# Even mixer reordered, output-norm sums moved to GpSimd, and a chunk-by-chunk first tile, in an eight-core decoder step

## The chip, the cores and the metric

The kernel runs as one program on all 8 NeuronCores of one Trainium2 chip (two dies, cores 0 to 3 and 4 to 7). Each core handles one prompt sequence of 2048 tokens and 16 sampled sequences of 8 tokens; nothing is exchanged between cores. The metric is the device time of the slowest core in microseconds (us), lower is better. Every execution also lists each core's span (first to last instruction) and the mean clock that the throttle granted to its TensorE.

Executions are labelled fast or slow. Slow means that one die was over 1% longer than the other at a lower clock, or that the run was over 1.5% above the fastest of the same kernel.

## The reference, cut to what matters

A trunk of two layers. Both have two SwiGLU half-steps and a gated per-layer embedding; layer 0 has the "even" mixer, layer 1 the "odd" one (a short gated convolution).

```python
def even_mixer(h, ...):
    proj = h @ w_in                     # xa (512) | va (512) | ga (512)
    pooled = causal_multiscale_pool(xa) # trailing means of 2, 4, 8, 16 rows, minus the row
    pa = einsum(pooled, pool_proj) * pool_scale
    u = va * sigmoid(ga)
    yb = silu(layernorm(causal_depthwise_conv(u, 31 taps) + dw_bias))
    return concat([pa, yb]) @ w_out
# for each layer
x = x + 0.5 * swiglu(rmsnorm(x), ...)
x = x + mixer(rmsnorm(x))
x = x + 0.5 * swiglu(rmsnorm(x), ...)
x = x + sigmoid(rmsnorm(x) @ w_ple_gate) * rmsnorm(p @ w_ple_proj)
```

## The kernel before

The tokens of a core are five blocks: 0 to 3 of 512 prompt tokens, and the "sample" block SB of 128. X (fp32), H (normed input, bf16) and the weights' ring stay in SBUF. The program is written in one stream: `defer(t, f)` puts work off until an estimated TensorE time, `ensure(tag)` runs what is pending now, and a scheduler derives the semaphores. `bank` hands out PSUM banks, `scr` and `SQ` hand out scratch. Cuts are marked with `# ...`.

```python
class Norm:                                # sums of squares of X for the next RMSNorm
    def chunk(self, mo, lag=0.8):          # called once for each of the 8 chunks of a block
        def square():
            if self.mode == "dve" and mo == 0:
                self.acc = scr(); act(self.acc, xs, AF.Square); return
            sq = SQ.get()
            act(sq, xs, AF.Square)
            defer((2.0 if self.mode == "pe" else 1.2) * k, lambda: add(sq), self.tag)
        def add(sq):                       # "pe": a matmul with ones; "dve": an add on VectorE
            # ...
            elif mo < 7:
                dve_tt(self.acc, self.acc, sq, ALU.add); SQ.put(sq)
            else:
                dve_tt(sq, self.acc, sq, ALU.add); sfree(self.acc)
                defer(2.5 if n == 512 else 9.0, lambda: stats(sq), self.tag)   # one matmul

def out_proj(b, src, wo, gnext):           # of both mixers
    nm = Norm(b, gnext)                    # mode "dve"
    for mo in range(8):
        pb = bank()
        mm(pb, [(wo[mo][:, k, :], src[b][:, k, :]) for k in range(8)])
        dve_tt(X[b][:, mo, :], pb, X[b][:, mo, :], ALU.add)
        nm.chunk(mo)

# inside even_mixer
def load_r(b):      # 16 DMAs: copies of u, shifted by 0 to 3 rows, for the convolution ("rr")
    # ... queue "act" if b > 1 and q % 2 else "sp"
def pp(b):          # pool_proj: one matmul a channel group, then a copy on ScalarE into H
    for c in range(4):
        mm(pb, [(wpp[:, c, :], H[b][:, c, :])])
        act(H[b][:, c, :], pb, AF.Copy, scale=pcol("pool_scale", c))

for b in (0, 1, 2, SB, 3):
    for j in range(4):
        vg(j, b)                           # value and gate, u
    xa(b)                                  # pool input; windowed sums on VectorE, 9 us a block
    # b == 0: load_r(0), states
    if b == SB:
        conv(0)
        load_r(1)
for b in range(NB):
    if b + 1 < NB:
        conv(b + 1)                        # conv + casts + LayerNorm statistics
    pp(b)
    if b + 2 < NB:
        load_r(b + 2)
    out_proj(b, H, wo, gnext)

# the start of the program
# X[0] on two queues; weight tile 0 waits for X chunk 2; X[1] waits for weight tile 2
for c in range(8):
    raw[0].chunk(c, "dve")                 # H = X * gain (unscaled), squares, statistics by matmul
def chunk1(c):
    raw[1].chunk(c, "pool")                # H of block 1 on GpSimd
for c in range(8):
    defer(9.5 + 0.75 * c, lambda c=c: chunk1(c), ("raw", 1))
# ffn then runs tiles 0..3 of block 0, tiles 0..3 of block 1, and so on
```

## Time and profile before

| | before |
|---|---|
| median of 4 runs | 2684.82 us (2683.16 to 2687.39) |
| profiled execution | 2663.17 us, slowest core 2661.4 |
| TensorE busy | 97% of the span |
| spans of the eight cores in the profiled execution | 2651.0 to 2661.4 us |

The page of the profile gives each engine's busy time (us, share of the span, instructions) and the chain of waits that ended last, as shares of the span by engine.

```profile
PE 2586.6 (97%) x14375; PEld 1249.3 (47%) x14375; DVE 1187.5 (45%) x2144; ACT 704.6 (26%) x1250; POOL 99.6 (4%) x174
...
PE 85%; DVE 8%; ACT 3%; issue 1%; DMA 1%; ACTq 0%; POOL 0%; SPq 0%; DVEq 0%; POOLq 0%
```

TensorE is busy for 97% of the span and is 85% of the chain, so it is the bottleneck: only its idle time and its time at a lower clock can be won back. Its timeline for the start of the slowest core (core 6) shows start, duration, operation, and in brackets the idle time before it with what ended it:

```profile
6.21 0.59 PE L547 MATMUL ps<-sq_88,ones 128*128 128x512 bf16 x1 [6.21 <-DVE h_48 L714]
...
15.94 14.53 PE L547 MATMUL ps<-h_48,ring 128*128 128x512 bf16 x56 [2.17 <-DMA ring<-wts]
...
34.25 0.39 PE L547 MATMUL ps<-sq_88,ones 128*128 128x512 bf16 x1 [0.48 <-ACT sq_88 L510]
38.81 3.59 PE L547 MATMUL ps<-h_49,ring 128*128 128x512 bf16 x8 [4.18 <-POOL h_49 L714]
...
60.20 1.90 PE L547 MATMUL ps<-h_50,ring 128*128 128x512 bf16 x8 [1.81 <-DVE h_50 L520]
```

Block 0's first tile begins at 15.94 us, when its weights have landed. Block 1 (h_49) waits 4.18 us for GpSimd's last chunk. Block 2 (h_50) is reached at 60.20 us.

The same view for the even mixer:

```profile
590.26 2.48 PE L547 MATMUL ps<-h_52,ring 128*128 128x128 bf16 x24 [3.39 <-DVE scr_95 L520]
...
632.52 1.04 PE L547 MATMUL ps<-pt_75,onesl 128*128 128x512 bf16 x2 [3.14 <-DVE pt_75 L534]
...
641.22 3.63 PE L547 MATMUL ps<-h_48,ring 128*128 128x512 bf16 x16 [1.64 <-ACT h_48 L510]
...
667.83 5.31 PE L547 MATMUL ps<-h_49,ring 128*128 128x512 bf16 x16 [1.98 <-ACT h_49 L510]
...
696.04 5.31 PE L547 MATMUL ps<-h_50,ring 128*128 128x512 bf16 x16 [2.08 <-ACT h_50 L510]
...
715.84 0.28 PE L547 MATMUL ps<-pt_75,onesl 128*128 128x128 bf16 x2 [2.24 <-DVE pt_75 L534]
...
721.60 3.60 PE L547 MATMUL ps<-h_51,ring 128*128 128x512 bf16 x8 [1.89 <-ACT h_51 L510]
...
741.93 6.44 PE L547 MATMUL ps<-h_52,ring 128*128 128x128 bf16 x64 [3.19 <-ACT h_52 L510]
```

Here TensorE waits for the sample block's gating on VectorE (scr_95), three times for casts of the convolution's output (pt_75; one of them, 0.84 us, is not shown), and before each output projection for ScalarE's pool copies (h_48 to h_52).

### The profile page before, as it was taken

To read this page: it belongs to the slowest core of one execution; us is meant where nothing else is said; L and a number is where in the kernel's file an instruction comes from. 1 tells how busy PE (TensorE), PEld (TensorE's weight loads), DVE (VectorE), ACT (ScalarE), POOL (GpSimd) and SP (SyncE) were. 2 spreads that over 40 slices of the span, in tenths; PEclk is the share of its full clock that TensorE was granted. 3 is DMA by queue.
4 is the path that set the end of the run, shared out by engine and by line. 5 is a ranking of instruction groups with operands and counts; after the bars stand their busy time and mean duration, and the time that the engine had idled before them with its cause. 6 is when DMAs were issued, how large, how long until landed. Compare 5 with 4: busy or idle time off the path is not lost.

```text
span 2661.4 us, 34887 instructions; the slowest of 8 cores (2651.0 to 2661.4 us)
## 1 busy us (share of the span) xinstructions
PE 2586.6 (97%) x14375; PEld 1249.3 (47%) x14375; DVE 1187.5 (45%) x2144; ACT 704.6 (26%) x1250; POOL 99.6 (4%) x174
## 2 busy tenths in 40 slices
PE   7999999999899999999999999999999999999997
PEld 2444544443354444444444454445444444544443
DVE  3432434765742222248832222257568322222587
ACT  5210112325531101124521001123333210011254
POOL 2000000000000000000000000000000000000000
PEclk9999999999899999999999999999999999999999
DMA  9220421145322204213032121202320221322113
GB/s 205 42 41 4 64 44 25 33 88 116 85 44 37 44 9 71 44 25 49 8 56 44 25 45 32 44 13 37 50 46 16 49 44 25 46 46 40 21 22 135
DMA packets 53312, 127.19 MB, mean 48 GB/s; under 512 B 9504, under 2 KB 24608, under 8 KB 53024
## 3 DMA queue, kind: packets, MB, share of 16 engines
q0 software_dynamic: 23584, 92.55, 21.4%
q1 hardware_dynamic: 25392, 27.90, 3.7%
q10 hardware_dynamic: 4176, 4.50, 0.7%
q8 instruction: 113, 1.85, 0.3%
q14 instruction: 47, 0.39, 0.0%
HBM read 196.61 MB, written 10.62 MB: 78 GB/s over the span
## 4 chain that ended last, share of the span: by engine, by line
PE 85%; DVE 8%; ACT 3%; issue 1%; DMA 1%; ACTq 0%; POOL 0%; SPq 0%; DVEq 0%; POOLq 0%
PE ps L547 85%; DVE h_50 L520 1%; ACT L508 1%; DVE h_51 L520 1%; DMA ring<-wts 1%; DMA xscr_69<-st_sc 0%; DVE x_46 L520 0%; DVE h_49 L520 0%; DVE v L516 0%; DVE h_48 L520 0%; DVE x_45 L520 0%; DVE x_43 L520 0%; DVE scr_97 L516 0%; DVE scr_96 L516 0%; DVE scr_96 L520 0%
## 5 line engine op out<-in xcount | busy, mean ns | idle before, releaser
L547 PE MATMUL ps<-h_49,ring 128*128 128x512 bf16 x1892 | 430.9, 382 | 6.2 <-POOL h_49 L714 4.2
L547 PE MATMUL ps<-h_48,ring 128*128 128x512 bf16 x1892 | 430.9, 382 | 6.1 <-DVE x_47 L516 2.3
L547 PE MATMUL ps<-h_50,ring 128*128 128x512 bf16 x1892 | 427.9, 380 | 5.3 <-ACT h_50 L510 2.1
L547 PE MATMUL ps<-h_51,ring 128*128 128x512 bf16 x1892 | 429.7, 381 | 2.0 <-ACT h_51 L510 1.9
L547 PEld LDWEIGHTS ps<-h_49,ring 128*128 128x128 bf16 x1892 | 185.8, 98 | 231.9 <-issue 5.2
L547 PEld LDWEIGHTS ps<-h_50,ring 128*128 128x128 bf16 x1892 | 185.3, 98 | 230.6 <-ACT h_50 L510 2.6
L547 PEld LDWEIGHTS ps<-h_51,ring 128*128 128x128 bf16 x1892 | 185.6, 98 | 227.4 <-issue 3.5
L547 PEld LDWEIGHTS ps<-h_48,ring 128*128 128x128 bf16 x1892 | 182.2, 98 | 211.9 <-issue 8.1
L571 POOL DMA_DIRECT2D ring<-wts x152 | 81.0, 540 | 2297.0 <-PE ps L547 2248.5
L547 PE MATMUL ps<-hid_54,ring 128*128 128x512 bf16 x736 | 163.7, 379 | 0.0
L547 PE MATMUL ps<-hid_55,ring 128*128 128x512 bf16 x736 | 163.7, 379 | 0.0
L547 PE MATMUL ps<-hid_56,ring 128*128 128x512 bf16 x736 | 163.7, 379 | 0.0
L547 PE MATMUL ps<-hid_53,ring 128*128 128x512 bf16 x736 | 162.8, 379 | 0.0
L510 ACT ACTIVATE scr_97<-ps 128x512 f32<-128x512 f32 (+1 forms) x128 | 72.7, 568 | 265.4 <-PE ps L547 263.4
L510 ACT ACTIVATE scr_95<-ps 128x512 f32<-128x512 f32 (+1 forms) x116 | 59.8, 515 | 311.1 <-PE ps L547 307.2
L510 ACT ACTIVATE scr_93<-ps 128x512 f32<-128x512 f32 (+1 forms) x128 | 73.6, 575 | 250.7 <-PE ps L547 240.3
L547 PE MATMUL ps<-h_52,ring 128*128 128x128 bf16 x1892 | 126.7, 223 | 9.7 <-DVE scr_95 L520 3.4
L547 PEld LDWEIGHTS ps<-h_52,ring 128*128 128x128 bf16 x1892 | 117.1, 100 | 32.5 <-DVE scr_95 L520 3.6
L510 ACT ACTIVATE scr_94<-ps 128x512 f32<-128x512 f32 (+1 forms) x108 | 54.3, 503 | 234.8 <-PE ps L547 229.7
L510 ACT ACTIVATE scr_96<-ps 128x512 f32<-128x512 f32 (+1 forms) x125 | 59.0, 472 | 207.6 <-PE ps L547 200.5
L547 PEld LDWEIGHTS ps<-hid_54,ring 128*128 128x128 bf16 x736 | 72.0, 98 | 86.9
L547 PEld LDWEIGHTS ps<-hid_56,ring 128*128 128x128 bf16 x736 | 72.1, 98 | 86.6
(474 smaller groups left out, 2161.5 us busy)
## 6 DMA issues: line engine op xcount, KB each, us to landing
ring<-wts POOLq DMA_DIRECT2D x110, 512.0 KB, 9.0
ring<-wts POOLq DMA_DIRECT2D x40, 768.0 KB, 7.9
rr<-u SPq DMA_DIRECT2D x36, 135.0 KB, 3.1
x_44<-xT SPq DMA_DIRECT2D x8, 256.0 KB, 5.8
x_45<-xT SPq DMA_DIRECT2D x8, 256.0 KB, 7.9
x_46<-xT SPq DMA_DIRECT2D x8, 256.0 KB, 9.5
yT<-x_43 SPq DMA_DIRECT2D x8, 256.0 KB, 2.1
yT<-x_44 SPq DMA_DIRECT2D x8, 256.0 KB, 2.1
```

The costliest lines, as they stand in the source:

```text
L508: e.preload_act_table_set(tset)
L510: return e.activation(out=out, in_=in_, func=func, **kw)
L520: S.op("dve", lambda e: e.scalar_tensor_tensor(out=out, in0=in0, scalar=scalar, in1=in1, op0=op0, op1=op1), reads=rd, writes=[out])
L547: ins = e.matmul(o_, l, r, start=st, stop=sp)
L571: S.op(eng, lambda e: e.dma_start(out=out, in_=in_), reads=[in_], writes=[out], dma_sem=sem, dma_total=total, extra_deps=extra)
```

## The change

Its intent: put VectorE's backlogs under projections that don't need them, take the norm sums of the output projections off VectorE, and start the first tile as X arrives.

```diff
@@ Norm: a third mode, sums on GpSimd; statistics in "pe" mode put off longer
+            self.wait = {"pe": 4.0, "dve": 1.2, "pool": 1.0}[mode]
+            add_tt = pool_tt if self.mode == "pool" else dve_tt
-                defer((2.0 if self.mode == "pe" else 1.2) * k, lambda: add(sq), self.tag)
+                defer(self.wait * k, lambda: add(sq), self.tag)
-                    dve_tt(self.acc[:, 0:n], self.acc[:, 0:n], sq[:, 0:n], ALU.add)
+                    add_tt(self.acc[:, 0:n], self.acc[:, 0:n], sq[:, 0:n], ALU.add)
@@ out_proj
-        nm = Norm(b, gnext)
+        nm = Norm(b, gnext, "dve" if b == SB else "pool")
@@ RawNorm.chunk: H of blocks 0 and 1 both on VectorE; squares kept in HID, statistics after the tile
-            S.op(eng, lambda e: e.tensor_scalar(out=H[b][:, c, :], ...
+            dve_ts(H[b][:, c, :], X[b][:, c, :], pcol(self.gname, c), ALU.mult)
@@ ffn: first tile of blocks 0 and 1 chunk by chunk
+                if rw is not None and pi == 0 and j == 0:
+                    for k in range(8):
+                        mm_ops([(pg[:, 0:n], wt[:, k, 0:128], H[b][:, k, :], k == 0, k == 7),
+                                (pu[:, 0:n], wt[:, k, 128:256], H[b][:, k, :], k == 0, k == 7)])
+                    rw.stats()
@@ even_mixer: load_r all on one queue, weights of pp loaded before diag, and this order
-        for b in (0, 1, 2, SB, 3):   ... vg, xa; conv(0), load_r(1) after SB
-        for b in range(NB):          ... conv(b + 1), pp(b), load_r(b + 2), out_proj(b)
+        vgs(0); xa(0); load_r(0)     # calls set on one line here
+        vgs(1); pp(0); xa(1)
+        vgs(2); pp(1)
+        vgs(SB); xa(2); xa(SB)
+        vgs(3, (0, 1)); conv(0); load_r(1); vgs(3, (2, 3))
+        xa(3); pp(2); pp(SB)
+        for b in range(NB):
+            if b + 1 < NB:
+                conv(b + 1)
+                if b + 2 < NB:
+                    load_r(b + 2)
+            if b == 0:
+                pp(3)
+            ensure(("ln", b))
+            out_proj(b, H, wo, gnext)
@@ start: weight tile 0 first; X[1] behind weight tile 1; tile order
-    W.extra[0] = (("x0_2", 0, 16),)
+    W.extra[1] = (("x0_3", 0, 16),)
+    W.extra[3] = (("x1_2", 0, 16),)
+    first = [(0, 0), (1, 0), (2, 0), (0, 1), (1, 1), (2, 1), (3, 0), (3, 1)]   # (tile, block)
```

More of the change, by code (lines that the diff above doesn't have):

```diff
@@ L77, in weight_tile_list @@
                 tiles.append((("ine_xa", j), 8 * 256))
+            tiles.append((("pp",), 4 * 128))
             tiles.append((("diag",), 16 * 8 * 32))
-            tiles.append((("pp",), 4 * 128))
             for ch in TRI:
@@ L516, in dve_tt, with pool_tt @@
         S.op("dve", lambda e: e.tensor_tensor(out=out, in0=in0, in1=in1, op=op), reads=[in0, in1], writes=[out])
+    def pool_tt(out, in0, in1, op):
+        S.op("pool", lambda e: e.tensor_tensor(out=out, in0=in0, in1=in1, op=op), reads=[in0, in1], writes=[out])
     def dve_stt(out, in0, scalar, in1, op0, op1):
@@ L592, in __init__ @@
             self.extra = {}
-            self.limit = 4
         def _place(self, k):
@@ L613, in _place, with pump @@
             return None if best is None else (best[1], u)
-        def pump(self):
-            while self.pos < self.limit:
+        def pump(self, limit=1 << 20):
+            while self.pos < min(limit, len(self.order)):
                 k = self.order[self.pos]
@@ L645, in __init__ @@
             self.tag = ("n", b)
-            self.pb = None
+            self.nsq = self.nadd = 0
+            self.wait = {"pe": 4.0, "dve": 1.2, "pool": 1.0}[mode]
         def chunk(self, mo, lag=0.8):
@@ L650, in chunk @@
             k = 1.0 if n == 512 else 0.4
+            add_tt = pool_tt if self.mode == "pool" else dve_tt
             def square():
-                if self.mode == "dve" and mo == 0:
+                self.nsq += 1
+                if self.mode != "pe" and self.nsq == 1:
                     self.acc = scr()
@@ L658, in square @@
                 act(sq[:, 0:n], xs, AF.Square)
-                defer((2.0 if self.mode == "pe" else 1.2) * k, lambda: add(sq), self.tag)
+                defer(self.wait * k, lambda: add(sq), self.tag)
             def add(sq):
+                i = self.nadd
+                self.nadd += 1
                 if self.mode == "pe":
-                    if mo == 0:
+                    if i == 0:
                         self.pb = bank()
-                    mm(self.pb[:, 0:n], [(ONES[:, :], sq[:, 0:n])], start=mo == 0, stop=mo == 7)
+                    mm(self.pb[:, 0:n], [(ONES[:, :], sq[:, 0:n])], start=i == 0, stop=i == 7)
                     SQ.put(sq)
-                    if mo == 7:
+                    if i == 7:
                         self.rsqrt()
-                elif mo < 7:
-                    dve_tt(self.acc[:, 0:n], self.acc[:, 0:n], sq[:, 0:n], ALU.add)
+                elif i < 6:
+                    add_tt(self.acc[:, 0:n], self.acc[:, 0:n], sq[:, 0:n], ALU.add)
                     SQ.put(sq)
                 else:
-                    dve_tt(sq[:, 0:n], self.acc[:, 0:n], sq[:, 0:n], ALU.add)
+                    add_tt(sq[:, 0:n], self.acc[:, 0:n], sq[:, 0:n], ALU.add)
                     sfree(self.acc)
-                    defer(2.5 if n == 512 else 9.0, lambda: stats(sq), self.tag)
+                    defer({512: 2.5, NSAMP: 9.0}[n] + (1.5 if self.mode == "pool" else 0.0), lambda: stats(sq), self.tag)
             def stats(sq):
@@ L708, in __init__, with chunk, stats, lead_order @@
             self.rs = RSB[b]
-            self.pb = None
-        def chunk(self, c, eng):
+        def chunk(self, c):
             n, b = self.n, self.b
-            col = pcol(self.gname, c)
-            S.op(eng, lambda e: e.tensor_scalar(out=H[b][:, c, :], in0=X[b][:, c, :], scalar1=col, scalar2=None,
-                                                op0=ALU.mult), reads=[X[b][:, c, :], col], writes=[H[b][:, c, :]])
-            sq = SQ.get()
+            sq = HID[SB - 1 - b][:, c, :]
+            dve_ts(H[b][:, c, :], X[b][:, c, :], pcol(self.gname, c), ALU.mult)
             act(sq[:, 0:n], X[b][:, c, :], AF.Square)
-            def add():
-                if c == 0:
-                    self.pb = bank()
-                mm(self.pb[:, 0:n], [(ONES[:, :], sq[:, 0:n])], start=c == 0, stop=c == 7)
-                SQ.put(sq)
-                if c == 7:
-                    act(self.rs[:, 0:n], self.pb[:, 0:n], AF.Abs_reciprocal_sqrt, bias=NORM_EPS)
-                    bfree(self.pb)
-            defer(1.6, add, ("raw", b))
-    def lead_order(nt, lead):
-        out = []
+        def stats(self):
+            n = self.n
+            pb = bank()
+            mm(pb[:, 0:n], [(ONES[:, :], HID[SB - 1 - self.b][:, c, 0:n]) for c in range(8)])
+            act(self.rs[:, 0:n], pb[:, 0:n], AF.Abs_reciprocal_sqrt, bias=NORM_EPS)
+            bfree(pb)
+    def lead_order(nt, lead, first=None):
+        out = list(first or [])
         for b in range(NB):
-            out += [(t, b) for t in range(min(lead, nt))]
+            out += [(t, b) for t in range(min(lead, nt)) if (t, b) not in out]
         for t in range(lead, nt):
@@ L790, in emb_stats, with ffn @@
         defer(0.6, s0, tag)
-    def ffn(l, f, gnext, lead=3, raw=()):
+    def ffn(l, f, gnext, lead=3, raw=(), first=None, arrive={}):
         for pi, part in enumerate(HPARTS):
@@ L796, in ffn @@
                     load_pt(l, b, b)
-            order, last = lead_order(len(part), lead if pi == 0 else 0)
+            order, last = lead_order(len(part), lead if pi == 0 else 0, first if pi == 0 else None)
             for oi, (j, b) in enumerate(order):
@@ L804, in ffn @@
                 pg, pu = bank(), bank()
-                mm(pg[:, 0:n], [(wt[:, k, 0:128], H[b][:, k, :]) for k in range(8)])
-                mm(pu[:, 0:n], [(wt[:, k, 128:256], H[b][:, k, :]) for k in range(8)])
+                pe_t[0] = max(pe_t[0], arrive.get((pi, j, b), 0.0))
+                if rw is not None and pi == 0 and j == 0:
+                    for k in range(8):
+                        mm_ops([(pg[:, 0:n], wt[:, k, 0:128], H[b][:, k, :], k == 0, k == 7),
+                                (pu[:, 0:n], wt[:, k, 128:256], H[b][:, k, :], k == 0, k == 7)])
+                        pe_t[0] += 2 * (n + 6.5) / 2400.0
+                    rw.stats()
+                else:
+                    mm(pg[:, 0:n], [(wt[:, k, 0:128], H[b][:, k, :]) for k in range(8)])
+                    mm(pu[:, 0:n], [(wt[:, k, 128:256], H[b][:, k, :]) for k in range(8)])
                 sg = scr()
@@ L885, in load_r @@
                         src = US[32 * q:32 * q + 32, :, s * NS:s * NS + L]
-                    items.append(("act" if b > 1 and q % 2 else "sp", RALL[32 * s:32 * s + 32, :, q, 0:L], src))
+                    items.append(("sp", RALL[32 * s:32 * s + 32, :, q, 0:L], src))
             dma_group(items, "rsem")
@@ L1029, in state, with vgs @@
                 dma("sp", V[:, :, 0:15 * NS], d_stp[:, :, :], "stp")
-        for b in (0, 1, 2, SB, 3):
+        def vgs(b, js=range(4)):
             ensure(("n", b))
@@ L1034, in even_mixer @@
                 ensure(("us",))
-            for j in range(4):
+            for j in js:
                 vg(j, b)
-            xa(b)
-            if b == 0:
-                dve_memset(RALL[96:128, :, :, 536:RW], 0.0)
-                load_r(0)
-                for j in range(4):
-                    defer(3.0 * j, lambda j=j: state(j), ("us",))
-                dma("sp", d_o_ps[:, :, 0:7 * NS], d_stp[:, :, 8 * NS:15 * NS], "osem")
-                dma("sp", d_o_ds[:, :, 0:22 * NS], d_stdw[:, :, 8 * NS:30 * NS], "osem")
-            if b == SB:
-                conv(0)
-                load_r(1)
+        vgs(0)
+        xa(0)
+        dve_memset(RALL[96:128, :, :, 536:RW], 0.0)
+        load_r(0)
+        for j in range(4):
+            defer(3.0 * j, lambda j=j: state(j), ("us",))
+        dma("sp", d_o_ps[:, :, 0:7 * NS], d_stp[:, :, 8 * NS:15 * NS], "osem")
+        dma("sp", d_o_ds[:, :, 0:22 * NS], d_stdw[:, :, 8 * NS:30 * NS], "osem")
+        wpp = kview(W.get(("pp",)), 4)
+        vgs(1)
+        pp(0)
+        xa(1)
+        vgs(2)
+        pp(1)
+        vgs(SB)
+        xa(2)
+        xa(SB)
+        vgs(3, (0, 1))
+        conv(0)
+        load_r(1)
+        vgs(3, (2, 3))
+        for j in range(4):
+            W.done(("ine_vg", j))
+        xa(3)
+        W.done(("ine_xa", 0))
+        W.done(("ine_xa", 1))
         dve_ts(O_DP[:, :, :], O_DP[:, :, :], 0.5, ALU.mult)
@@ L1050, in even_mixer @@
         dma("sp", d_o_pp[:, :, :], PTAIL[:, :, 1:16], "osem")
-        for j in range(4):
-            W.done(("ine_vg", j))
-        W.done(("ine_xa", 0))
-        W.done(("ine_xa", 1))
-        wpp = kview(W.get(("pp",)), 4)
+        pp(2)
+        pp(SB)
         wo = out_tiles("oute")
@@ L1059, in even_mixer @@
                 conv(b + 1)
-            else:
+                if b + 2 < NB:
+                    load_r(b + 2)
+            if b == 0:
+                pp(3)
+                W.done(("pp",))
+            if b + 1 == SB:
                 W.done(("diag",))
-            pp(b)
-            if b + 2 < NB:
-                load_r(b + 2)
             ensure(("ln", b))
             out_proj(b, H, wo, gnext)
-        W.done(("pp",))
         for ch in TRI:
@@ L1148, in ple @@
             W.done(("pleg", l, ch))
+    W.pump(1)
     dma("act", PAR[:, :], d_par[:, :], "psem")
@@ L1155, in build_program @@
             dma("act" if b == 0 and c % 2 else "sp", X[b][:, c, :], d_xT[:, o_:o_ + n], f"x{b}_{c}",
-                extra=(("wsem4", 0, 16),) if b == 1 and c == 0 else ())
-    W.extra[0] = (("x0_2", 0, 16),)
+                extra=(("wsem2", 0, 16),) if b == 1 and c == 0 else ())
+    W.extra[1] = (("x0_3", 0, 16),)
+    W.extra[3] = (("x1_2", 0, 16),)
     W.extra[4] = tuple((f"x{SB}_{c}", 0, 16) for c in range(8))
-    dve_memset(ONES[:, :], 1.0 / D)
+    W.pump()
     raw = [RawNorm(b, "norm_ffn00") for b in range(2)]
     for c in range(8):
-        raw[0].chunk(c, "dve")
-        pe_t[0] += 0.8
-        run_due()
-    pe_t[0] = 11.5
+        raw[0].chunk(c)
+        if c == 0:
+            dve_memset(ONES[:, :], 1.0 / D)
     dve_memset(ONESL[:, :], 1.0 / 512)
@@ L1170, in build_program, with at_time @@
         dve_memset(RC[:, t:t + 1], 1.0 / (t + 1))
-    W.pump()
-    def chunk1(c):
-        raw[1].chunk(c, "pool")
-        if c == 7:
-            W.limit = len(wtiles)
-            W.pump()
+    pe_t[0] = 9.4
+    def at_time(t, fn, tag):
+        defer(t - pe_t[0], fn, tag)
     for c in range(8):
-        defer(9.5 + 0.75 * c, lambda c=c: chunk1(c), ("raw", 1))
+        at_time(19.5 + 0.87 * c, lambda c=c: raw[1].chunk(c), ("raw", 1))
     n0 = [Norm(b, "norm_ffn00", "pe" if b < SB else "dve") for b in range(NB)]
     for b in range(2, NB):
+        n0[b].wait = 1.5
         for mo in range(8):
-            defer((16.0, 24.0, 32.0)[b - 2] + (0.7, 0.9, 0.5)[b - 2] * mo, lambda b=b, mo=mo: n0[b].chunk(mo, 0.0), ("n", b))
+            at_time((27.0, 37.0, 47.0)[b - 2] + (0.8, 1.0, 0.5)[b - 2] * mo,
+                    lambda b=b, mo=mo: n0[b].chunk(mo, 0.0), ("n", b))
+    first = [(0, 0), (1, 0), (2, 0), (0, 1), (1, 1), (2, 1), (3, 0), (3, 1)]
+    arrive = {(0, 1, 0): 15.5, (0, 2, 0): 18.5, (0, 3, 0): 28.5}
     for l in range(2):
-        ffn(l, 0, f"norm_mix{l}", lead=4 if l == 0 else 3, raw=raw if l == 0 else ())
+        if l == 0:
+            ffn(l, 0, f"norm_mix{l}", lead=4, raw=raw, first=first, arrive=arrive)
+        else:
+            ffn(l, 0, f"norm_mix{l}")
         if l == 0:
```

## The prediction

The forecast's sum came to 11 + 24 + 3 = 38 us (steps 1 to 3), less some for a wait not foreseen, and gave 2650 us.

> **What bounds it now.** TensorE: busy 97% of 2661.4 us on the slowest core and 85% of the chain that ended last. So the change can win back only TensorE's idle and half-clock time. At the warm start-to-start time of 0.216 us per 512-column matmul (0.056 for 128 columns) all matmuls need about 2560 us; some 89 us on this core is lost, by the matmuls' starts: 26.6 us before 80 us, 40.1 in the even mixer (500 to 770 us; 33 to 45 over the cores), 9.4 around 1300 us (untouched), 8.3 in and after the odd output projection, 12.1 at the end (untouched).
>
> - Start (timeline of TensorE): first matmul at 6.21, statistics matmuls until 13.2, weights at 15.94, a 4.18 us wait for POOL's h_49 at 38.81; block 2 starts at 60.20.
> - Mixer: 0.52 and 3.39 us for the sample's evacuations behind VectorE's work on xa(2); 0.84, 3.14, 2.24 us for the convolution's casts; 1.64, 1.98, 2.08, 1.89, 3.19 us for ScalarE's pool copies h_48..h_52 right before each out_proj. Together 20.9 us.
> - Clock: long gaps are followed by 3.4 to 10 us at 0.5. [...] 34 us of it in the mixer, costing up to half that.
>
> **What the change does.**
> 1. Start: weights first; gate and up matmuls follow each X chunk; statistics after the tile. First tile done near 13.5 instead of 20 us. H of block 1 moves from POOL (1604 ns a chunk) to VectorE (about 0.5 us). Block 2 should start near 48 us. Gain about 11 us.
> 2. Mixer: pp(b) no longer stands directly before its out_proj: its 10.8 us of waits go, with their half clock. The sample's projections precede xa(2): 3.9 us go. But conv(0) now follows xa(2) and xa(sample), about 9 + 6 us of VectorE work over 9 us of TensorE work, and conv(1) still follows xa(3) closely: I expect 2 to 4 us of wait for casts at each. Loss 37 to about 13: gain about 24 us.
> 3. Norm sums: 7 adds a block leave VectorE (0.68 us each) for GpSimd. [...] The 1.12 us waits for sums (2032, 2048 us) and part of the 2.25 us bank wait at 2061 should go: about 3 us.
>
> Sum 38 us, on TensorE's critical path, so it counts in full; I take off some for a wait not foreseen.
>
> **Predicted** 2650 us (1.4% less), range 2634 to 2670. Faster by over 2% needs 54 us, nearly all that is lost in touched places: 0.07. Within 2%: 0.92. Slower: 0.01.
>
> **Right or wrong, in the profile:** block 2's first matmul at 44 to 52 us; no wait on h_48..h_52 before out_proj; cast waits at conv(0) and conv(1) small but present; half-clock time in the mixer below 17 us; [...] lost time from 89 to about 50.
>
> **What would make it wrong:** GpSimd adds over 2 us, or queued behind its weight loads (waits for sums appear); the xa backlog stalling conv(0) by 5 us or more; X's first chunks landing later [...].

## More of the kernel before

Last, groups of VectorE instructions in the second half of the even mixer (count, then busy us and mean ns of one); they matter later:

```profile
L516 DVE TENSOR_TENSOR v<-v,scr_96 128x512 f32<-128x512 f32 x12 | 7.5, 682 | 0.0
L516 DVE TENSOR_TENSOR v<-v,ps 128x512 f32<-128x512 f32 x12 | 7.4, 679 | 0.0
...
L534 DVE CAST pt_75<-v 128x512 bf16<-128x512 f32 x4 | 1.7, 424 | 0.4 <-ACT v L510 0.3
```

## The result

| | before | after |
|---|---|---|
| median | 2684.82 us | 2652.57 us (2650.53 to 2654.95, 4 runs) |
| ratio of the fast runs | | 0.9882, 95% interval 0.9863 to 0.9902 |
| slowest core of the profiled execution | 2661.4 us | 2653.2 us |

A ratio here and below is the mean time of one kernel's fast runs over that of the other's fast runs of the same rounds, so it is not quite the ratio of the medians quoted.

2652.6 us against a predicted 2650: the number held. But the timed runs gained 32 us and the profiled executions only 8. Something in the timed runs of before is not in its profile. The profile after, in the same views. The page:

```profile
PE 2578.3 (97%) x14375; PEld 1250.3 (47%) x14375; DVE 1175.1 (44%) x2096; ACT 708.6 (27%) x1252; POOL 157.7 (6%) x222
...
PE 88%; DVE 6%; DMA 2%; ACT 2%; issue 1%; SPq 0%; POOL 0%; ACTq 0%; DVEq 0%; POOLq 0%
```

The start, on its slowest core (core 4):

```profile
12.80 6.11 PE L550 MATMUL ps<-h_48,ring 128*128 128x512 bf16 x16 [12.80 <-DMA ring<-wts]
...
21.57 7.08 PE L550 MATMUL ps<-h_48,ring 128*128 128x512 bf16 x32 [0.94 <-DMA ring<-wts]
...
34.93 1.89 PE L550 MATMUL ps<-h_49,ring 128*128 128x512 bf16 x4 [1.18 <-DVE h_49 L528]
...
59.33 1.90 PE L550 MATMUL ps<-h_50,ring 128*128 128x512 bf16 x8 [1.53 <-DVE h_50 L523]
```

The first tile is spread over 12.80 to 18.7 us, the wait for h_49 has shrunk to pieces of about 1 us, but block 2 is reached at 59.33 us on this core, hardly earlier than before. Core 4 is the latest of the eight here: over all cores the same view has block 2 at 53.89 to 59.33 us, against 58.47 to 60.78 us before, about 4 us earlier in the median.

The even mixer:

```profile
623.42 0.23 PE L550 MATMUL ps<-h_52,ring 128*128 128x128 bf16 x1 [1.53 <-ACT scr_95 L510]
...
633.29 8.21 PE L550 MATMUL ps<-rr,ring 128*32 128x512 bf16 x96 [7.93 <-DMA rr<-u]
...
690.57 0.60 PE L550 MATMUL ps<-pt_75,onesl 128*128 128x512 bf16 x2 [2.22 <-DVE pt_75 L537]
...
716.02 0.39 PE L550 MATMUL ps<-pt_75,onesl 128*128 128x128 bf16 x2 [5.88 <-DVE pt_75 L537]
...
718.52 0.61 PE L550 MATMUL ps<-sq_92,ones 128*128 128x512 bf16 x1 [1.14 <-POOL sq_92 L519]
...
739.67 6.23 PE L550 MATMUL ps<-h_52,ring 128*128 128x128 bf16 x64 [3.71 <-ACT h_52 L510]
```

The four waits on h_48 to h_51 and the wait of the sample's gating are gone. In their place stand a wait of 7.93 us for the shifted copies of u (rr) at conv(1), four waits up to 1.5 us for pool evacuations at pp(SB) (one shown), a longer wait for a cast (5.88 instead of 2.24 us) and two for GpSimd's sums (1.14 us on sq_92 and a shorter one). The wait on h_52 stays (3.71 against 3.19 us). The groups of VectorE instructions that answer to those of before:

```profile
L516 DVE TENSOR_TENSOR v<-v,scr_95 128x512 f32<-128x512 f32 x12 | 10.6, 937 | 0.0
L516 DVE TENSOR_TENSOR v<-v,ps 128x512 f32<-128x512 f32 x12 | 7.4, 675 | 0.0
...
L537 DVE CAST pt_75<-v 128x512 bf16<-128x512 f32 x5 | 3.8, 752 | 5.5 <-ACT v L510 5.5
```

Subtract and multiply of the LayerNorm with both inputs in SBUF (v and scr) take 937 ns instead of 682; the one with a PSUM input is unchanged (675 against 679 ns); the casts take longer too (752 instead of 424 ns; the other buffer's, pt_77, 524 instead of 427). In the timeline of this core the slow ones lie beside GpSimd's adds: three casts at 663 to 667 us, while adds of 1.16 us run almost without a break, take 1.31, 1.01 and 0.99 us, and the next one at 669.27 us, with no add running, takes 0.43. The GpSimd adds themselves, two of their groups:

```profile
L519 POOL TENSOR_TENSOR scr_93<-scr_93,sq_88 128x512 f32<-128x512 f32 x4 | 5.2, 1300 | 7.5 <-ACT sq_88 L510 7.0 <-POOL scr_93 L519 0.2
...
L519 POOL TENSOR_TENSOR sq_92<-scr_97,sq_92 128x512 bf16<-128x512 f32 x1 | 1.7, 1665 | 0.6 <-ACT sq_92 L510 0.6
```

### The profile page after: what moved, and what is told of

Same layout as the page of the kernel before. It is cut to its first block, busy times and chain, and to the rows that moved or that the text cites. A ratio compares the mean times of both kernels' runs of the same rounds, so it can differ in the third digit from the quotient of the medians.

```text
span 2653.2 us, 34986 instructions; the slowest of 8 cores (2636.8 to 2653.2 us)
## 1 busy us (share of the span) xinstructions
PE 2578.3 (97%) x14375; PEld 1250.3 (47%) x14375; DVE 1175.1 (44%) x2096; ACT 708.6 (27%) x1252; POOL 157.7 (6%) x222
## 4 chain that ended last, share of the span: by engine, by line
PE 88%; DVE 6%; DMA 2%; ACT 2%; issue 1%; SPq 0%; POOL 0%; ACTq 0%; DVEq 0%; POOLq 0%
PE ps L550 88%; DVE h_50 L523 1%; ACT L508 1%; DMA ring<-wts 1%; DMA rr<-u 1%; SPq L574 0%; DMA x_43<-xT 0%; DVE h_49 L523 0%; DVE h_48 L523 0%; DVE x_46 L523 0%; DVE x_45 L523 0%; DVE x_43 L523 0%; DMA x_44<-xT 0%; DVE scr_96 L523 0%; DVE x_44 L523 0%
## 6 DMA issues: line engine op xcount, KB each, us to landing
x_46<-xT SPq DMA_DIRECT2D x8, 256.0 KB, 12.5
```

## The experiments

Twelve kernels were run, four at a time, with the kernel before interleaved in each set. All gave correct results. The second and the third set ran on the same chip.

### First set: the change taken apart

Edits: `p1_start_only` is the kernel before with the start, tile order, `RawNorm` and `ffn` parts of the diff alone (it also keeps after's order of the pp and diag weights); `p2_mixer_only` with the even mixer's order and `load_r` alone; `p3_pool_only` with GpSimd's sums alone; `p4_pewait_only` with this alone (shortened):

```diff
-                defer((2.0 if self.mode == "pe" else 1.2) * k, lambda: add(sq), self.tag)
+                defer((4.0 if self.mode == "pe" else 1.2) * k, lambda: add(sq), self.tag)   # embedding norms only
```

> Only the new start (weights of the first tile before X, gate and up matmuls chunk by chunk, block 1's H on VectorE, new tile order) on the kernel before. Theory A, the sums of lost TensorE time in the two profiles (26.6 us before, about 22 after in the first 80 us): 4 to 5 us faster than the kernel before, ratio 0.998. Theory B, the timed runs of before (2684 us) lose 20 us more than its profiled run (2663 us) in one place, and the part that touches that place wins it back: if that place is the start, 20 to 27 us faster, ratio 0.990 to 0.993.

> Only the reordered even mixer (with its load_r all on one queue and pp's weights before diag) on the kernel before. Theory A (lost time 38 us before, 36 after between 500 and 770 us): 0 to 5 us faster, ratio 0.998 to 1.000, and a wait of 2 to 9 us of TensorE for the shifted copies of u (rr) at conv(1) as in the profile after. Theory B with the mixer as the place: 20 to 27 us faster, 0.990 to 0.993. My prediction had said 24 us.

> Only the norm sums of both out_proj on GpSimd. Theory A (lost time in 1860 to 2100 us 5.7 before, 1.9 after): 3 to 4 us faster, ratio 0.9985. Theory B with this part as the place: 20 us or more faster. GpSimd adds of 1.15 to 1.5 us each.

> Only the longer deferral (4.0 instead of 2.0) of the statistics matmuls in the per-layer embedding. Theory A: lost time there 9.4 before and 8.5 to 10 after at 1300 us, 12.1 and 10 at the end with a tail 2 us longer: within 2 us of before, ratio 1.000. Theory B: not this part.

Now that each run lists its cores, the puzzle resolves. In the profiled execution of `p3_pool_only` two cores stand out (span and mean granted clock of a core):

```profile
core 5: 2657.3 us, clock 0.991
core 6: 2687.9 us, clock 0.981
core 7: 2683.3 us, clock 0.981
```

Both kinds of core ran the same program. Busy time by stretch for core 5 (stretch; busy us and count of TensorE, weight loads, VectorE, ScalarE, GpSimd; granted clock; DMA share; GB/s):

```profile
60.00:200.00 140.00, 139.78 (x779) 68.63 (x778) 58.32 (x101) 31.84 (x60) 4.76 (x9) 1.00 0.28 47
220.00:500.00 280.00, 280.00 (x1495) 134.98 (x1493) 121.31 (x191) 47.80 (x83) 7.94 (x15) 1.00 0.19 32
```

and for core 6:

```profile
60.00:200.00 140.00, 139.54 (x641) 63.26 (x640) 51.21 (x90) 29.67 (x55) 3.72 (x7) 0.81 0.26 44
220.00:500.00 280.00, 280.00 (x1506) 135.50 (x1505) 106.39 (x167) 40.81 (x73) 8.48 (x16) 1.00 0.20 34
```

Between 60 and 200 us core 6 is granted 0.81 of the clock and gets 641 matmuls done where core 5 does 779; from 220 us on both run at 1.00. The trace's clock records of core 6 have one stretch of 13/16 (0.8125) from 47.8 us, 161.4 us long; core 7 has the same, cores 0 to 5 have none. The cores of such a pair lose about 26 us. Wherever a profile of this set has such a stretch, it begins at 47.5 to 48.9 us, lasts 161 to 162 us, and takes cores 0-1, 2-3, 4-5 or 6-7 together (in the profile of `p2_mixer_only` all four pairs: mean clocks of 0.981 to 0.983 on all eight cores). In executions without a profile I count a fast run as "hit" when cores have a mean clock under 0.9865:

| set 1, fast runs | hit | median | undisturbed runs | median span of the cores not hit |
|---|---|---|---|---|
| before | 7 of 9 | 2685.8 | 2659.9, 2662.1 | 2655.6 |
| `p1_start_only` | 0 of 4 | 2654.7 | all | 2649.9 (-5.7) |
| `p2_mixer_only` | 3 of 3 | 2676.6 | none | 2646.7 (-8.9) |
| `p3_pool_only` | 4 of 4 | 2689.1 | none | 2658.9 (+3.3) |
| `p4_pewait_only` | 3 of 6 | 2674.0 | 2660.9 to 2661.7 | 2656.2 (+0.6) |
| after (its own four runs) | 0 of 4 | 2652.6 | all | 2645.2 (-10.4) |

(The last column is the median over all cores of fast runs that kept the full clock, in brackets against before; ratios of the fast runs: 0.9908, 0.9992, 1.0033 and 0.9981. Slow runs are left out: 2 of before, 1 of `p1`, 4 of `p2`, 2 of `p3`; the two later sets had 20 among their 71 runs.) Theory B is right for the start: that part alone brings the time to 2654.7 us. Of its 31 us only about 6 are work done sooner; the rest is the 13/16 clock that it does not run into. On undisturbed cores the four parts add up (-5.7 - 8.9 + 3.3 + 0.6 = -10.7) to what after shows (-10.4). The mixer's order alone is worth 9 us, and the GpSimd sums cost 3.

`p2_mixer_only` on its slowest core shows where the mixer's expected gain went:

```profile
PE ps L547 <- DMA rr<-u: 8.4, 1, 8.4
PE ps L547 <- DVE pt L534: 5.4, 3, 3.5
PE ps L547 <- ACT scr L510: 3.3, 4, 1.5
PE ps L547 <- ACT h L510: 2.6, 1, 2.6
```

The new wait for rr belongs to the new order (0.4 to 8.4 us on the four cores I read); the waits for casts are 5.4 us without GpSimd's sums, against 9.6 in after.

### Second set: what sets off the 13/16 clock, and two mixer costs

`p5_before_h1_dve` is the kernel before with

```diff
-        raw[1].chunk(c, "pool")
+        raw[1].chunk(c, "dve")
-        defer(9.5 + 0.75 * c, lambda c=c: chunk1(c), ("raw", 1))
+        defer(10.5 + 1.0 * c, lambda c=c: chunk1(c), ("raw", 1))
```

> The kernel before with one thing of the new start: H of block 1 made by VectorE instead of GpSimd, so that the 4.2 us wait before block 1's first matmul (and the half clock behind it, then full clock with all cores starting together) goes. Theory G (the 13/16 clock of about 161 us that sets in at 48 us on one or more pairs of cores is set off by that restart from the gap): no 0.8125 stretch in any execution, median 2657 to 2661 us against 2686. Rival H (set off by something else of the old start, as the data traffic or the dense run of tiles): 0.8125 stretches on at least one pair in most executions as before (9 of 11), median 2680 or more.

Measured: 2658.49 us median of all 7 runs; fast runs 2655.7 to 2658.5, ratio 0.9919 (0.9869 to 0.9969). 0 of 4 fast runs were hit, while before was hit in 7 of 9 in the same rounds. The undisturbed work gained 2.8 us (median core, as in the table's last column, 2652.2 against 2655.0). So this edit, a changed engine and the start times that go with it, keeps the 13/16 clock away about as the whole new start does. Four fast runs are few, but at before's rate of 7 in 9 four such runs in a row would be rare (an estimate: about once in 400). Three further runs were slow and are left out. (The "9 of 11" above counts all runs of before but the two undisturbed ones, so two slow ones too.)

The edit did less to TensorE than I expected. In its profile block 1 still starts at 36.9 to 38.7 us (before: 37.8 to 39.8). The one long wait for GpSimd, 3.3 to 4.6 us in before's profile, has become waits of at most 2.3 us between statistics matmuls, and seven of the eight cores still run 3.4 to 6.8 us at half clock in the first 100 us (in before all eight do). So neither some idle time nor a restart at half clock went away; what went is GpSimd's work on block 1 and the unbroken gap.

`p6_after_h1_pool` is the kernel after with

```diff
-            dve_ts(H[b][:, c, :], X[b][:, c, :], pcol(self.gname, c), ALU.mult)
+            S.op("pool" if b == 1 else "dve", lambda e: e.tensor_scalar(... same operands ...))
```

> The kernel after with one thing of the old start: H of block 1 made by GpSimd (1.6 us a chunk instead of 0.5), which brings a wait of several us before block 1's tiles back. Theory G: the 0.8125 stretches come back in most executions, 2672 us or more. Rival H: none comes back; 2 to 6 us slower than after (2652) from the wait alone.

Measured: 2686.18 us, ratio 1.0026, but not for the reason named. The profile has no 0.8125 stretch. In after, weight loads that wait for the sample's X stand ahead of these chunks in GpSimd's queue (here five went out at 51.53 us, after a wait of 23.43 us for X, and the chunks ran from 54.18 us), and TensorE waited 27.55 us for the first one:

```profile
55.85 1.04 PE L550 MATMUL ps<-h,ring 128*128 128x512 bf16 x2 [27.55 <-POOL h L721]
```

and the eight cores ran 34 to 38 us at half clock in the first 100 us. The experiment is confounded; it says nothing about the 13/16 clock, except that a long gap with a sparse restart did not set it off in the execution profiled.

`p7_after_even_dve` is the kernel after with

```diff
-        nm = Norm(b, gnext, "dve" if b == SB else "pool")
+        nm = Norm(b, gnext, "dve" if b == SB or src is H else "pool")   # src is H: even mixer
```

> The kernel after with the norm sums of the even mixer back on VectorE, those of the odd mixer on GpSimd as in after. Theory P (GpSimd's adds slow VectorE's operations with two SBUF inputs, 682 to 937 ns, and its casts, so that TensorE waits longer for the convolution's casts): waits for the casts 9.6 down to about 5.4 us, the two-input subtract and multiply back at 0.68 us, 3 to 6 us faster than after: 2647 to 2650 us. Rival Q (moving the sums off VectorE helps or is neutral): same or slower than after.

Measured: fast runs 2645.3 to 2648.2 us, none hit, median core 2641.1 us against after's 2645.2. Waits for casts 5.5 us on two of the three cores read (4.2 us and 2.5 us of a related wait on the third), the wait for rr still 5.5 to 6.4 us, and the two groups are back where they were:

```profile
L516 DVE TENSOR_TENSOR v<-v,scr 128x512 f32<-128x512 f32 x12 | 7.5, 682 | 0.0
...
L537 DVE CAST pt<-v 128x512 bf16<-128x512 f32 x9 | 3.8, 426 | 9.1 <-ACT v L510 7.0 <-PE ps L550 2.0
```

Theory P holds. (After itself was not among this set; its 2652.6 us is from four undisturbed runs, and the undisturbed runs of before agree between the first two sets: 2659.7 to 2662.1 us.)

`p8_after_rr_first` is the kernel after with

```diff
+    W.extra[W.order.index(("oute", TRI[1]))] = (("rsem", 0, 16 * 32),)   # wait for both load_r
```

> The kernel after with the second and later weight loads of the out projection held until the shifted copies of u for block 1 have landed. Theory D (the new order lets those weight loads start while the last copies are in flight; the copies then take 14 us instead of 3 to 5 and conv(1) waits for them): the wait for rr at conv(1) (1.6 to 8.8 us on the eight cores) goes, last copies land in under 7 us, 3 to 8 us faster than after: 2645 to 2650 us. Rival E (the copies are simply issued too late, 12 us of issue on one queue): the wait stays above 3 us on most cores.

Measured: fast runs 2643.6 to 2647.2 us, none hit, median core 2640.4 us. The last four copies for block 1 (line of the DMA issues: count, KB each, median us to landing), in after:

```profile
rr<-u SPq DMA_DIRECT2D x4, 134.8 KB, 13.9
```

in before:

```profile
rr<-u SPq DMA_DIRECT2D x4, 134.8 KB, 5.4
```

and here:

```profile
rr<-u SPq DMA_DIRECT2D x4, 134.8 KB, 3.2
```

GpSimd's queue on core 4 shows the weight loads, first of after, where two go out at 613.73 us, among the copies (issued 605.0 to 616.9 us):

```profile
613.73 1.06 POOL L574 DMA_DIRECT2D ring<-wts  x2 [20.47 <-PE ps L550]
```

then of this kernel, where they follow the copies:

```profile
616.44 2.13 POOL L574 DMA_DIRECT2D ring<-wts  x4 [25.84 <-DMA rr<-u]
```

No wait for rr is left on the cores I read. Theory D holds and E falls: the copies are not issued too late, they are held up by the weight loads.

### Third set: gap, density or GpSimd; and both corrections

`p9_after_dense_block1` makes after's first tile of block 1 of two whole accumulations; `p10_before_h1_dve_gap` is `p5` with six adds before the last chunk; `p11_before_chunked_block1` makes before's first tile of block 1 chunk by chunk.

```diff
# p9 (on after)
+                if rw is not None and pi == 0 and j == 0 and b == 1:
+                    mm(pg[:, 0:n], [(wt[:, k, 0:128], H[b][:, k, :]) for k in range(8)])
+                    mm(pu[:, 0:n], [(wt[:, k, 128:256], H[b][:, k, :]) for k in range(8)])
+                    rw.stats()
# p10 (on p5)
+        if c == 7:
+            for _ in range(6):
+                dve_tt(t[:, 0:512], t[:, 0:512], t[:, 0:512], ALU.add)
# p11 (on before)
+                if rw is not None and pi == 0 and j == 0 and b == 1:
+                    for k in range(8):
+                        mm_ops([... gate and up of chunk k ...])
```

> The kernel after, but block 1's first tile as two whole accumulations that wait for all of H of block 1, instead of chunk by chunk. No work on GpSimd. TensorE then idles some 6 us (28.5 to about 35 us) and restarts with dense matmuls. Theory G (an idle gap that ends in a dense restart on all cores sets off the 13/16 clock of 161 us): 0.8125 stretches, near 45 us, on at least one pair in most executions, 2672 us or more. Rival S (GpSimd's work at the same time was needed for it): none, 2651 to 2656 us.

> The kernel before with block 1's H on VectorE as in the earlier run, and six idle-work adds of 0.69 us before its last chunk, so that the gap before block 1 is as long as before or longer while GpSimd does no arithmetic. Theory G: 0.8125 stretches back in most executions, median 2680 to 2692. Rival S: none, 2659 to 2665 us.

> The kernel before, GpSimd still making block 1's H, but block 1's first tile chunk by chunk, so that TensorE restarts sparsely (2 matmuls per 1.6 us) instead of densely after the gap. Theory G: far fewer or no 0.8125 stretches, median near 2658 to 2663. Rival S: stretches as before, median 2683 or more.

Measured: medians of the fast runs 2659.7, 2661.2 and 2658.6 us (2660.2, 2661.5 and 2659.9 over all runs; ratios 0.9989, 0.9996, 0.9988), no fast run hit. But in this set the kernel before was hit in 0 of its 8 fast runs as well (2660.0 to 2665.2 us), on the same chip on which it had been hit in 7 of 9 in the set before. So these three say nothing about what sets the clock off; they are inconclusive. What they do give is an undisturbed cost: a dense first tile of block 1 costs after some 7 us (2659.7 us, the median of its fast runs, against 2652.6, which was measured in another set).

`p12_after_both` has the edits of `p7` and `p8`:

> The kernel after with both corrections: even mixer's norm sums on VectorE, and the later output projection weights held behind the shifted copies of u. If they add: waits for casts 5.5 us, no wait for rr at conv(1), 8 to 14 us faster than after: 2639 to 2644 us, the fastest of all. If they share a wait: 2644 to 2647, no better than either alone.

Measured: 2642.17 us, fast runs 2641.0 to 2642.9, ratio 0.9924 (0.9910 to 0.9938) to a kernel before that was not hit either. That is 10.4 us below after's median (after was not in this set, and its runs and these were undisturbed), inside the range expected if the corrections add. They add nearly, not fully: the median core is 8.0 us below after's (2637.25 against 2645.2), where `p7` and `p8` alone had 4.1 and 4.8. TensorE's waits in the mixer of its slowest core:

```profile
PE ps L550 <- DVE pt L537: 5.3, 3, 3.5
PE ps L550 <- ACT scr L510: 3.5, 4, 1.5
PE ps L550 <- ACT h L510: 3.0, 2, 2.6
PE ps L550 <- DVE sq L516: 2.4, 2, 1.7
```

No wait for rr is left, and casts cost 5.3 us. This is the fastest version, and it beats both kernels.

## Why the prediction was right or wrong

**The time** (2650 against 2652.6 measured) was right by luck: the sum behind it was not. I had 11 + 24 + 3 us of TensorE work won back, less a little. The undisturbed cores show 10.4 us in all (the median core; the slowest core of an undisturbed run gained about 8). Accordingly, the lost time of the slowest core in the profiles fell by 8 us, not by the 39 forecast (both kernels run the same 14375 matmuls), and GpSimd's busy time rose by 58 us (99.6 to 157.7). About 24 us of the measured 32 are a cost that I had not seen: in 14 of 18 fast runs of the first two sets the kernel before lost some 26 us on one or two pairs of cores to a 13/16 clock, and none of the 4 runs of after did. The four runs of before that the result is taken against came without their cores' clocks, but lie at 2683.2 to 2687.4 us, where every hit run of the first two sets lies (2683.1 to 2688.6), and none of the undisturbed (2659.7 to 2665.2). The hint was there: the profiled execution was 20 us or more shorter than all timed ones.

**Step 1, the start ("Gain about 11 us", "First tile done near 13.5", "Block 2 should start near 48 us")** was mis-sized: `p1_start_only` gains 5.7 us on undisturbed cores, the first tile ends at 18.7 us on after's slowest core, and block 2 starts at 53.9 to 59.3 us over its cores, some 4 us earlier than before in the median, not 12. The failed term is X's arrival, which I had named as a risk. Tile 0's weights were issued at 1.55 us and landed only at 12.80 us; with them in flight, X's last chunks came near 14.8 instead of 12.4 us (VectorE's work on them in the two timelines; median times to landing of X's chunks 8.6 and 11.7 us on the two queues instead of 5.7 and 7.7). The second weight tile waits for X's fourth chunk and was issued only at 13.71 us, and X of block 1, behind it, at 21.60 instead of 22.12 us on the slowest cores (18.96 to 22.03 against 21.23 to 22.56 us over all eight). Block 1's data was asked for only about a microsecond sooner, so block 2 could not come 12 us sooner. This is read from the timelines; no run changed the order of these loads alone.

**Step 2, the mixer ("Loss 37 to about 13: gain about 24 us")** failed. The named waits did go: the sample's gating, and h_48 to h_51. h_52 stayed (3.71 us). Waits for casts "small but present" were 5.4 us in all in `p2` (6.2 in before), and 9.6 with GpSimd's sums in after. What I had not counted: the wait for rr at conv(1), 1.6 to 8.8 us over the cores of after, because the new order frees the ring for weight loads while the copies are in flight (`p8` removes it), and four waits of up to 1.5 us, together 3.3 us in `p2`, at pp(SB), which now stands right behind xa(3). Half-clock time in the mixer was predicted below 17 us; it was 17 to 31 us. The order alone gains 8.9 us.

**Step 3, the sums ("about 3 us")** had the wrong sign. GpSimd's adds took 1.15 to 1.67 us, within the 1.73 us between output-projection chunks, and in the odd projection, from which I had taken the 3 us, TensorE's waits fell from 5.9 to 1.7 us (1860 to 2100 us, slowest cores). But I had left out what they do to VectorE. In the trace its subtract and multiply with two SBUF inputs went from 682 to 937 ns, those with one in PSUM stayed at 679 and 675 ns. The casts, which have one input, slowed too (424 to 752 ns); by what mechanism, no trace here shows. In the even mixer those very instructions release the convolution. `p3_pool_only` costs 3.3 us, and undoing it for the even mixer gains 4.1 (median cores). The loss is in the even mixer: in `p3` its waits for casts are 10.5 to 12.5 us on three cores against 5.4 to 6.2 on the same cores of before, and 2.3 us for GpSimd's last sum come on top.

**The clock.** Shown: the stretch is in the old start's executions and not in the new one's; in the first two sets 24 of 31 fast runs of kernels that make block 1's H on GpSimd in the old start (before, `p2`, `p3`, `p4`) were hit, and 0 of 17 of those that make it on VectorE (`p1`, `p5`, `p7`, `p8`); moving that work to VectorE suffices (`p5`, four fast runs). Not settled: why. A dense restart of all cores after the one unbroken gap of some 4 us, or GpSimd's work beside TensorE's, would both fit, and the runs meant to tell them apart fell in a time when even the kernel before was spared. What makes the chip prone at one time and not at another is open too, and the slow runs, which eleven of the twelve experiments and before had (all but `p4`), are not explained here. One of them is telling: in the slowest of `p8` (3147.37 us) all four cores of one die had a mean clock of 0.811 to 0.812, about 13/16 over the whole run.

## What to carry to other kernels

Before working on a kernel, compare the profiled execution with the timed ones, core by core: if they differ, part of the time is not in the profile, and one kernel can be "faster" only because it keeps the clock (here about 24 of 32 us). When work is moved to GpSimd, look at which of VectorE's instructions have two SBUF inputs (here 682 to 937 ns; the casts suffered too, 424 to 752) and run at the same time, for they can pay for it. When an order frees buffers earlier, ask which loads that starts and what they will collide with (here copies of 135 KB took 13.9 us beside weight loads and 3.2 us with those held back).
